# A four-layer hybrid denoising step on one core: 128-row contraction in every sample score matmul, and two layers' modulation vectors made in the retention layer

## The chip, the core and the metric

The kernel runs on one core of a Trainium2 chip. The metric is the device time of one execution in microseconds (us). The engines are TensorE (PE for matmuls, PEld for its weight loads), VectorE (DVE), ScalarE (ACT), GpSimd (POOL) and SyncE (SP, which here only issues DMAs).

## What is computed

Five token tiles of 128 rows (four of the sample, one of the prompt) go through four layers of width 1024: differential attention, retention, HGRN2, differential attention. Cut to what the change touches, the reference reads:

```python
def modulation(cvec, w, b):                       # once per layer and conditioning vector
    m = jax.nn.silu(cvec) @ w + b
    shift, scale, gate = jnp.split(m, 3, axis=-1)

def block(qblk):                                  # differential attention, 16 sub-heads of 64
    s = jnp.einsum('bqsd,bksd->bsqk', qblk, k)
    p = jax.nn.softmax(s, axis=-1).reshape(B, H, 2, Q_BLOCK, -1)
    a = p[:, :, 0] - lam * p[:, :, 1]
    return jnp.einsum('bhqk,bkhe->bqhe', a, v)

for l in range(DEPTH):
    h = rms_norm(x, g_pre[l]) * (1.0 + scale) + shift
    y = mixer[l % 3](h)
    x = x + gate * rms_norm(y, g_post[l])
```

Sample queries attend to 512 own keys and 128 cached keys (640 in all), after a rotary embedding; prompt queries attend to the 128 prompt keys.

## The kernel before

**Split products.** Matmul operands in the fp32r type carry only part of an fp32 number, so every operand is cut into a high and a low part (`whi`/`wlo`, `hh`/`hl`, `kh`/`kl`), and a product is three matmuls: high by high, high by low, low by high. `proj_b` (L248 to L250) makes 128 output columns for 320 tokens in 24 such matmuls, twice per column; `narrow` (L223 to L225) and `wide_unit` (L456 to L458) make 256 and 512 columns.

**Attention layers (0 and 3).** For each of 8 heads `diff_part` makes keys, then queries (`rope`, then `use` with L754 to L761: DVE, POOL, then an ACT copy of the high part at L760 and a DVE subtraction for the low part at L761). Each head has two sub-heads of 64 rows. Four SP DMAs (L732) copy `kh` into `kk`, which has a sub-head's 64 rows twice, one above the other; four more (L739) build `qq`, the sub-head's high part and low part stacked. So one 128-row matmul (L781) gives two of the three products. The third, high part of q by low part of k, is a 64-row matmul (L784). Per head and sample tile there are, for each sub-head, two of the one and two of the other (320 keys each), eight in all; 8 heads, 4 tiles and 2 layers make 64 such groups of eight. DVE takes the row maximum (L785), ACT the exponential (L787), and after `combine` PE turns the result (L811) and multiplies by v (L821). The prompt's scores (L793) have a form of their own.

`kh` and `q` are separate tiles with one buffer each; `kl`, `kk` and `qq` have two. The cached keys of all heads come by one 512 KB DMA per layer (`ck`, L665).

**Order.** PE's order is written by hand. `weave` runs a mixing generator (`diff_mix`, `ret_mix`, `hg_mix`) and a filling one (the next head's projections, then `tail`); each yields a number, and the filler is advanced until its numbers make up for the mixer's. A scheduler lays out the other engines, each of which then works in order. In `ret_mix` the yields between the stages are `RW` = 3.5, 9 and 11; in `hg_mix` they are 6, 1.5, 6, 1.5, 4 and 4.

**Modulation.** A layer's 3072 values for two conditioning vectors are 12 blocks of 256 columns (0 to 3 shift, 4 to 7 scale, 8 to 11 gate). A block is two DMAs of 512 KB (`mraw`, L312) and eight rows; a row is two operations, an ACT copy for the first row of the block (L357) and a DVE multiply-add for the others (L359, 14 per block), except that in attention layers every second row goes to ACT and POOL. `mod_turn` (L327 to L337) then turns the block on PE and finishes it with some small DVE operations into `modT`. Rows are called from `weave` at `mod_pace` rows per unit of filling: four times the loads queued for the layer, over `PACE[kind]`. In each layer the queue `modq` holds that layer's own gate blocks and the next layer's shift and scale blocks: 12 blocks in layers 0, 1 and 2, 4 in layer 3. `mod_finish` in `tail` does what is left. `modT` has two buffers.

Of the kernel before, what the change touches and what calls it, by code (L numbers as in the profile page):

```python
# [11 lines left out]
F32 = mybir.dt.float32  # L12
F32R = mybir.dt.float32r
# [8 lines left out]
P = 128  # L22
D = 1024
# [15 lines left out]
RW = (3.5, 9.0, 11.0, 0.5)  # L39
PACE = (155.0, 245.0, 195.0)  # L40
TOK = (0, 128, 384, 512, 256)

# [44 lines left out]
class Net:  # L87
# [227 lines left out]
    def mod_turn(self):  # L315

        nc = self.nc
        if self.modp is None:
            return
        l, b, acc = self.modp  # L320
        self.modp = None
        if b == 0:
            self.mods[l] = self.cp.tile([P, 24, 2], F32, tag="modT", bufs=2, name="modT")
        ps = self.one([P, 2, 2, P])
        for c in range(2):
            for j in range(2):
                nc.tensor.transpose(ps[:, c, j, :], acc[:, j, c * 128:c * 128 + 128], self.ident)  # L327
        r = slice(2 * b, 2 * b + 2)
        m = self.mods[l][:, r, :]
        wide = lambda a: a.unsqueeze(2).to_broadcast([P, 2, 2])  # L330
        nc.vector.tensor_reduce(out=m, in_=ps, axis=AX.X, op=ALU.add)
        nc.vector.tensor_tensor(out=m, in0=m, in1=wide(self.bmodT[:, l, r]), op=ALU.add)
        if 4 <= b < 8:
            nc.vector.tensor_scalar(out=m, in0=m, scalar1=1.0, scalar2=None, op0=ALU.add)
        if b >= 4:
            g = (self.gpre if b < 8 else self.gpost)[:, l, b % 4 * 2:b % 4 * 2 + 2]
            nc.vector.tensor_tensor(out=m, in0=m, in1=wide(g), op=ALU.mult)  # L337
# [305 lines left out]
    def diff(self, l, y):  # L643
# [3 lines left out]
        with tc.tile_pool(name=f"da{l}", bufs=2, reuse_waits="tile") as mp:  # L647
# [15 lines left out]
            nc.vector.tensor_scalar(out=nlam, in0=nlam, scalar1=-lam_init, scalar2=None, op0=ALU.add)  # L663
            ck = mp.tile([P, D], F32, bufs=1, name="ck")
            nc.sync.dma_start(ck, t["cache_k"][0, j].rearrange("s h d -> s (h d)"))  # L665
            st = types.SimpleNamespace(mp=mp, l=l, j=j, cc=cc, cs=cs, sub=sub, nlam=nlam, v={}, sg={}, ck=ck, q={}, k={})
            st.o, st.scored, st.done = {}, -1, -1
# [16 lines left out]
    def diff_part(self, st, kind, p):  # L684
# [27 lines left out]
        else:  # L712
            h = p
            kh = mp.tile([P, 640], F32R, tag="kh", bufs=1, name="kh")
            kl = mp.tile([P, 640], F32R, tag="kl", name="kl")
            kp = mp.tile([P, NP], F32, tag="kp", name="kp")

            def cached():
                pt = self.one([P, P])
                nc.tensor.transpose(pt, st.ck[:, h * 128:h * 128 + 128], self.ident)  # L720
                nc.scalar.activation(kh[:, 0:128], pt, AF.Copy)
                self.lo(kl[:, 0:128], pt, kh[:, 0:128], nc.vector)
# [4 lines left out]
            if h == 0:  # L727
                cached()
            kk = mp.tile([P, 2, 640], F32R, tag="kk", name="kk")
            for s in range(2):  # L730
                for r in range(2):
                    nc.sync.dma_start(kk[64 * r:64 * r + 64, s, :].bitcast(F32), kh[64 * s:64 * s + 64, :].bitcast(F32))  # L732
            q = mp.tile([P, 2, NS], F32R, tag="q", bufs=1, name="q")
            qp = mp.tile([P, NP], F32, tag="qp", name="qp")
# [9 lines left out]
            nc.sync.dma_start(t["new_k"][0, j].rearrange("s h d -> s (h d)")[:, h * 128:h * 128 + 128], ko)  # L744
            st.q[h], st.k[h] = (qq, qp), (kk, kl, kp)

# [19 lines left out]
    def diff_mix(self, st, y):  # L766
        nc, mp = self.nc, st.mp

        def scores(h, tt):
            (qq, qp), (kk, kl, kp) = st.q[h], st.k[h]  # L770
            nm = mp.tile([P, 2], F32, tag="nm", name="nm")
            sums = st.o[h][2][:, tt, :]
            pr = []
            if tt < 4:
                for s in range(2):
                    rows = slice(64 * s, 64 * s + 64)
                    sc = self.two()
                    qc = slice(tt * 128, tt * 128 + 128)
                    for c in range(2):
                        kc = slice(c * 320, c * 320 + 320)  # L780
                        nc.tensor.matmul(sc[:, c, :320], qq[:, s, qc], kk[:, s, kc], start=True, stop=False)  # L781
                    for c in range(2):
                        kc = slice(c * 320, c * 320 + 320)
                        nc.tensor.matmul(sc[:, c, :320], qq[rows, s, qc], kl[rows, kc], start=False, stop=True)  # L784
                    nc.vector.tensor_reduce(out=nm[:, s:s + 1], in_=sc[:, :, :320], axis=AX.XY, op=ALU.max, negate=True)  # L785
# [475 lines left out]
    def start(self, src):  # L1261
        nc, t = self.nc, self.t
        mm, tr = nc.tensor.matmul, nc.tensor.transpose
        mt = self.mods[0] = self.cp.tile([P, 24, 2], F32, tag="modT", bufs=2, name="modT")
        with self.tc.tile_pool(name="in0", bufs=1, reuse_waits="tile") as ip:
# [100 lines left out]
    def layers(self, depth):  # L1366
# [14 lines left out]
        for l in range(depth):  # L1381
# [3 lines left out]
            else:  # L1385
                self.x_out = [self.dp.tile([P, D], F32, tag=f"x{l}_{tt}", name=f"x{l}_{tt}") for tt in range(NT)]
            self.modq += [(l, b, i) for b in range(8, 12) for i in range(2)]
            if l + 1 < depth:
                self.modq += [(l + 1, b, i) for b in range(8) for i in range(2)]
            self.mod_pace, self.mod_pool = 4 * (len(self.modq) + len(self.modr)) / PACE[kind], None  # L1390
# [42 lines left out]
```

## Time and profile before

| what | value |
|---|---|
| median of 3 runs | 1962.97 us (1962.2 to 1963.04) |
| the profiled execution, its own time | 1961.53 us |
| its span, first to last instruction | 1959.7 us |
| PE busy | 1869.7 us, 95% |
| DVE busy | 1322.9 us, 68% |
| ACT busy, POOL busy | 982.8 us, 50%; 495.0 us, 25% |
| mean granted TensorE clock | 0.984 |

By their matmuls the layers lie at about 20 to 480 us (attention), 480 to 1060 (retention), 1060 to 1530 (HGRN2) and 1530 to 1960 (attention). A busy time is the time in which at least one instruction of the engine was under way; matmuls overlap, so the distance between two starts, not the duration, is what one matmul costs in a stream.

### The profile page before, as it was taken

The numbers are of one execution on the slowest core, as the hardware profiler recorded it, in microseconds if no ns is written. First come the engines' busy times: TensorE is split into PE (matmuls) and PEld (weight loads), VectorE is DVE, ScalarE is ACT, GpSimd is POOL, SyncE is SP. The second block draws the span as 40 slices with busy tenths as digits, with TensorE's granted clock in tenths as the row PEclk, the third lists the DMA queues.
The fourth block names the chain that finished last, engine by engine and source line by source line (L and its number), as shares of the span: only waits on it lengthen the run. The fifth ranks groups of instructions, "written<-read, shape, count | busy, mean of one in ns | idle before, by whom it ended". The sixth has DMA issues, their size and how long they took to land.

```text
span 1959.7 us, 31888 instructions
## 1 busy us (share of the span) xinstructions
PE 1869.7 (95%) x12060; PEld 1664.0 (85%) x12060; DVE 1322.9 (68%) x2553; ACT 982.8 (50%) x2271; POOL 495.0 (25%) x419
## 2 busy tenths in 40 slices
PE   6999999999899999999999999999889999999998
PEld 3789889977788888898787999999877889999976
DVE  4768788757766666544248788989765757666654
ACT  3556666555534434334334555555554545554552
POOL 0424343202222222222003232323221612211101
PEclk9999999999999999999999999999889999999999
DMA  9534444314343333223323333333214433323212
GB/s 301 163 109 116 115 124 130 91 56 151 124 131 110 120 120 115 83 65 124 119 77 120 102 91 103 103 103 103 83 43 158 136 100 94 87 80 84 81 52 101
DMA packets 224824, 214.08 MB, mean 109 GB/s; under 512 B 10416, under 2 KB 198688, under 8 KB 224672
## 3 DMA queue, kind: packets, MB, share of 16 engines
q1 hardware_dynamic: 224208, 211.67, 36.0%
q8 instruction: 95, 1.56, 0.3%
q14 instruction: 57, 0.47, 0.1%
q10 hardware_dynamic: 464, 0.39, 0.1%
HBM read 174.79 MB, written 18.35 MB: 99 GB/s over the span
## 4 chain that ended last, share of the span: by engine, by line
PE 71%; DVE 14%; ACT 4%; issue 4%; DMA 3%; POOL 2%; SPq 1%; DVEq 0%; POOLq 0%; ACTq 0%
PE one L456 8%; PE one L458 8%; PE one L457 8%; PE one L248 6%; PE one L249 6%; PE one L250 6%; DVE macc L359 3%; PE one L223 3%; PE one L821 3%; PE one L225 3%; PE two L784 3%; PE one L224 3%; PE two L781 2%; DVE wlo L114 2%; PE one L811 1%
## 5 line engine op out<-in xcount | busy, mean ns | idle before, releaser
L248 PE MATMUL one<-hh,whi 128*128 128x320 f32 x1152 | 372.2, 323 | 13.1 <-ACT qp L757 7.0
L249 PE MATMUL one<-hl,whi 128*128 128x320 f32 x1152 | 360.2, 313 | 0.0
L250 PE MATMUL one<-hh,wlo 128*128 128x320 f32 x1152 | 359.9, 312 | 0.0
L114 DVE TENSOR_TENSOR wlo<-raw,whi 128x1024 fp32r<-128x1024 f32 x192 | 245.2, 1282 | 135.3 <-ACT whi L176 133.8
L456 PE MATMUL one<-whi,hh 128*128 128x512 f32 x744 | 301.1, 405 | 3.4 <-ACT yo L552 2.4
L458 PE MATMUL one<-whi,hl 128*128 128x512 f32 x744 | 295.3, 397 | 0.5 <-DVE hl L114 0.5
L457 PE MATMUL one<-wlo,hh 128*128 128x512 f32 x744 | 295.7, 397 | 0.0
L176 ACT ACTIVATE whi<-raw 128x1024 fp32r<-128x1024 f32 x192 | 201.6, 1056 | 154.7 <-PE one L249 51.5
L359 DVE SCALAR_TENSOR_TENSOR macc<-mraw,smod,macc 128x256 f32<-128x256 f32 x432 | 233.2, 576 | 9.6 <-POOL macc L361 9.5
L248 PEld LDWEIGHTS one<-hh,whi 128*128 128x128 f32 x1152 | 220.9, 192 | 21.2 <-ACT qp L757 7.4
L249 PEld LDWEIGHTS one<-hl,whi 128*128 128x128 f32 x1152 | 220.8, 192 | 0.5
L250 PEld LDWEIGHTS one<-hh,wlo 128*128 128x128 f32 x1152 | 220.5, 191 | 0.3 <-DVE wlo L114 0.3
L223 PE MATMUL one<-whi,hh 128*128 128x256 f32 x720 | 212.4, 295 | 0.0
L225 PE MATMUL one<-whi,hl 128*128 128x256 f32 x720 | 203.1, 282 | 0.0
L224 PE MATMUL one<-wlo,hh 128*128 128x256 f32 x720 | 202.2, 281 | 0.0
L456 PEld LDWEIGHTS one<-whi,hh 128*128 128x128 f32 x744 | 140.8, 189 | 37.2 <-ACT yo L552 2.9
L458 PEld LDWEIGHTS one<-whi,hl 128*128 128x128 f32 x744 | 140.2, 188 | 35.3 <-DVE hl L114 2.1
L457 PEld LDWEIGHTS one<-wlo,hh 128*128 128x128 f32 x744 | 140.8, 189 | 29.8
L361 POOL TENSOR_TENSOR macc<-macc,mpart 128x512 f32<-128x512 f32 x64 | 93.7, 1466 | 191.8 <-ACT macc L357 75.8
L223 PEld LDWEIGHTS one<-whi,hh 128*128 128x128 f32 x720 | 135.8, 189 | 5.7 <-issue 4.2
L389 POOL TENSOR_TENSOR rs<-ms,mhalf 128x1 f32<-128x1 f32 (+1 forms) x72 | 65.9, 916 | 287.4 <-DVE ms L382 155.4
L224 PEld LDWEIGHTS one<-wlo,hh 128*128 128x128 f32 x720 | 136.5, 190 | 0.0
(344 smaller groups left out, 3709.9 us busy)
## 6 DMA issues: line engine op xcount, KB each, us to landing
mraw<-in_w_mod SPq DMA_DIRECT2D x96, 512.0 KB, 3.8
raw<-in_da_w_in SPq DMA_DIRECT2D x56, 512.0 KB, 4.2
raw<-in_hg_w_in SPq DMA_DIRECT2D x36, 512.0 KB, 4.0
raw<-in_ret_w_in SPq DMA_DIRECT2D x64, 256.0 KB, 3.1
kk<-kh SPq DMA_DIRECT2D x64, 160.0 KB, 3.6
qq<-q SPq DMA_DIRECT2D x64, 128.0 KB, 3.2
raw<-in_da_w_out SPq DMA_DIRECT2D x16, 512.0 KB, 4.0
raw<-in_ret_w_in SPq DMA_DIRECT2D x16, 512.0 KB, 3.9
```

The source lines that it names most:

```text
L114: return (eng or self.nc.gpsimd).tensor_tensor(out=out, in0=full, in1=hi.bitcast(F32), op=ALU.subtract)
L176: self.nc.scalar.activation(hi, raw, AF.Copy)
L223: mm(out, xh, wh[:, k % 4, :], start=(first and k == ks[0]), stop=False)
L224: mm(out, xh, wl[:, k % 4, :], start=False, stop=False)
L225: mm(out, xl, wh[:, k % 4, :], start=False, stop=(last and k == ks[-1]))
L248: nc.tensor.matmul(ps, wh[:, k, :], self.hh[:, k, c], start=(k == 0), stop=False)
L249: nc.tensor.matmul(ps, wh[:, k, :], self.hl[:, k, c], start=False, stop=False)
L250: nc.tensor.matmul(ps, wl[:, k, :], self.hh[:, k, c], start=False, stop=(k == KT - 1))
L359: nc.vector.scalar_tensor_tensor(out=m, in0=raw[:, k, :], scalar=c, in1=m, op0=ALU.mult, op1=ALU.add)
L456: mm(ps, xh, wh, start=(first and k == ks[0]), stop=False)
L457: mm(ps, xh, wl, start=False, stop=False)
L458: mm(ps, xl, wh, start=False, stop=(last and k == ks[-1]))
```

## The change

Five edits. The low part of k is stacked as the high part was: `kh` and `kl` become the halves of one tile `ks`, and four more DMAs per head make `kz`, the low part's 64 rows twice. The third product becomes a 128-row matmul of the whole `qq` by `kz` (it now also adds the low part of q by the low part of k), and the order within a sub-head is `kk`, `kz`, `kk`, `kz`. `ks` and `q` share one buffer (tag "split"). The cached keys come head by head (64 KB each, two buffers). The table `MOD_IN` puts 24 blocks into layer 1 (its own gate, all of layer 2, shift and scale of layer 3), none into layer 2 and layer 3's gate into layer 3; layer 0 is as before. `modT` gets a third buffer, and the space kept for DMA descriptors is set smaller.

```diff
+MOD_IN = (((0, range(8, 12)), (1, range(8))), ((1, range(8, 12)), (2, range(8)), (2, range(8, 12)), (3, range(8))), (),
+          ((3, range(8, 12)),))
...
-            self.mods[l] = self.cp.tile([P, 24, 2], F32, tag="modT", bufs=2, name="modT")
+            self.mods[l] = self.cp.tile([P, 24, 2], F32, tag="modT", bufs=3, name="modT")
...
-            kh = mp.tile([P, 640], F32R, tag="kh", bufs=1, name="kh")
-            kl = mp.tile([P, 640], F32R, tag="kl", name="kl")
+            ck = mp.tile([P, P], F32, tag="ck", name="ck")
+            nc.sync.dma_start(ck, t["cache_k"][0, j].rearrange("s h d -> s (h d)")[:, h * 128:h * 128 + 128])
+            ks = mp.tile([P, 2, 640], F32R, tag="split", bufs=1, name="ks")
+            kh, kl = ks[:, 0, :], ks[:, 1, :]
...
-            kk = mp.tile([P, 2, 640], F32R, tag="kk", name="kk")
-            for s in range(2):
-                for r in range(2):
-                    nc.sync.dma_start(kk[64 * r:64 * r + 64, s, :].bitcast(F32), kh[64 * s:64 * s + 64, :].bitcast(F32))
-            q = mp.tile([P, 2, NS], F32R, tag="q", bufs=1, name="q")
+            kk, kz = (mp.tile([P, 2, 640], F32R, tag=n, name=n) for n in ("kk", "kz"))
+            for both, src in ((kk, kh), (kz, kl)):
+                for s in range(2):
+                    for r in range(2):
+                        nc.sync.dma_start(both[64 * r:64 * r + 64, s, :].bitcast(F32), src[64 * s:64 * s + 64, :].bitcast(F32))
+            q = mp.tile([P, 2, NS], F32R, tag="split", bufs=1, name="q")
...
                     for c in range(2):
                         kc = slice(c * 320, c * 320 + 320)
                         nc.tensor.matmul(sc[:, c, :320], qq[:, s, qc], kk[:, s, kc], start=True, stop=False)
-                    for c in range(2):
-                        kc = slice(c * 320, c * 320 + 320)
-                        nc.tensor.matmul(sc[:, c, :320], qq[rows, s, qc], kl[rows, kc], start=False, stop=True)
+                        nc.tensor.matmul(sc[:, c, :320], qq[:, s, qc], kz[:, s, kc], start=False, stop=True)
...
-            self.modq += [(l, b, i) for b in range(8, 12) for i in range(2)]
-            if l + 1 < depth:
-                self.modq += [(l + 1, b, i) for b in range(8) for i in range(2)]
+            for m, bs in MOD_IN[l]:
+                if m < depth:
+                    self.modq += [(m, b, i) for b in bs for i in range(2)]
...
-    nc = _bacc.Bacc("TRN2", target_bir_lowering=False, num_devices=1)
+    nc = _bacc.Bacc("TRN2", target_bir_lowering=False, num_devices=1, dynamic_dma_scratch_size=1024)
```

PE, the first sample tile's scores of the first head in layer 0, between two projection matmuls. Before:

```order
L250 MATMUL one<-hh,wlo 128x320
L781 MATMUL two<-kk,qq 128x320 x2
L784 MATMUL two<-kl,qq 128x320 x2
L781 MATMUL two<-kk,qq 128x320 x2
L784 MATMUL two<-kl,qq 128x320 x2
L248 MATMUL one<-hh,whi 128x320
```

After:

```order
L252 MATMUL one<-hh,wlo 128x320
L783 MATMUL two<-kk,qq 128x320
L784 MATMUL two<-kz,qq 128x320
L783 MATMUL two<-kk,qq 128x320
L784 MATMUL two<-kz,qq 128x320
L783 MATMUL two<-kk,qq 128x320
L784 MATMUL two<-kz,qq 128x320
L783 MATMUL two<-kk,qq 128x320
L784 MATMUL two<-kz,qq 128x320
L250 MATMUL one<-hh,whi 128x320
```

The number of matmuls is the same; the two kinds now alternate, and all eight read 128 rows.

ACT, the start of layer 0, from head 0's queries on (`q` is the query's high part, `ko` the new key for the output, `kh<-one` or `ks<-one` head 1's cached keys, `kp` and `qp` the prompt's parts, `mpart` modulation). Before:

```order
L757 ACTIVATE qp<-one 128x64
L357 ACTIVATE mpart<-mraw,smod 128x256 x2
L760 ACTIVATE q<-t_745 128x256
L176 ACTIVATE whi<-raw 128x1024
L743 ACTIVATE ko<-one 128x128
L357 ACTIVATE mpart<-mraw,smod 128x256
L757 ACTIVATE qp<-one 128x64
L357 ACTIVATE mpart<-mraw,smod 128x256
L721 ACTIVATE kh<-one 128x128
L357 ACTIVATE mpart<-mraw,smod 128x256 x2
L760 ACTIVATE q<-t_785 128x256
L757 ACTIVATE kp<-one 128x64
```

After:

```order
L359 ACTIVATE mpart<-mraw,smod 128x256 x2
L178 ACTIVATE whi<-raw 128x1024
L746 ACTIVATE ko<-one 128x128
L359 ACTIVATE mpart<-mraw,smod 128x256
L760 ACTIVATE qp<-one 128x64
L359 ACTIVATE mpart<-mraw,smod 128x256 x3
L763 ACTIVATE q<-t_749 128x256
L763 ACTIVATE q<-t_789 128x256
L760 ACTIVATE kp<-one 128x64
L178 ACTIVATE whi<-raw 128x1024
L760 ACTIVATE kp<-one 128x64
L723 ACTIVATE ks<-one 128x128
```

Both writes of `q` have moved behind what stood after the first of them, and head 1's cached keys have moved behind both.

DVE, one head in the middle of the retention layer, from the last product of the scores to the state update (`s` from `cd` and `one`). Before:

```order
L359 SCALAR_TENSOR_TENSOR macc<-mraw,smod,macc 128x256 x2
L114 TENSOR_TENSOR vl<-one,vh 128x256
L359 SCALAR_TENSOR_TENSOR macc<-mraw,smod,macc 128x256
L619 SCALAR_TENSOR_TENSOR sg<-sg,one 128x256
L114 TENSOR_TENSOR vl<-one,vh 128x256
L619 SCALAR_TENSOR_TENSOR sg<-sg,one 128x256
L1021 SCALAR_TENSOR_TENSOR s_6574<-s_5831,cd,one 128x256 x2
```

After:

```order
L116 TENSOR_TENSOR vl<-one,vh 128x256
L361 SCALAR_TENSOR_TENSOR macc<-mraw,smod,macc 128x256 x3
L621 SCALAR_TENSOR_TENSOR sg<-sg,one 128x256
L361 SCALAR_TENSOR_TENSOR macc<-mraw,smod,macc 128x256 x4
L333 TENSOR_REDUCE modT<-one 128x4
L116 TENSOR_TENSOR vl<-one,vh 128x256
L361 SCALAR_TENSOR_TENSOR macc<-mraw,smod,macc 128x256
L334 TENSOR_TENSOR modT<-modT,par 128x4
L361 SCALAR_TENSOR_TENSOR macc<-mraw,smod,macc 128x256 x2
L621 SCALAR_TENSOR_TENSOR sg<-sg,one 128x256
L361 SCALAR_TENSOR_TENSOR macc<-mraw,smod,macc 128x256 x5
L1021 SCALAR_TENSOR_TENSOR s_6699<-s_5877,cd,one 128x256 x2
```

Where three multiply-adds of the modulation stood ahead of the state update, fifteen stand now. Counted over the five heads from the second to the sixth table of decays, DVE's order holds 140 such multiply-adds (30, 26, 28, 28, 28) and 28 small `modT` operations before, 271 (57, 55, 52, 57, 50) and 56 after, with some 43 other operations per head in both. In the HGRN2 layer none are left.

## Rows read from the trace of the kernel before

**Rows 1.** The page, section 1: busy us (share of the span) and instructions.

```profile
span 1959.7 us, 31888 instructions
PE 1869.7 (95%) x12060; PEld 1664.0 (85%) x12060; DVE 1322.9 (68%) x2553; ACT 982.8 (50%) x2271; POOL 495.0 (25%) x419
```

**Rows 2.** Stretches: length, busy PE, PEld, DVE, ACT, POOL; granted clock, DMA share, GB/s.

```profile
120.00:400.00 280.00, 275.83 (x1982) 252.58 (x1982) 222.57 (x467) 175.54 (x492) 99.89 (x79) 1.00 0.40 113
540.00:790.00 250.00, 249.17 (x1436) 221.31 (x1435) 169.20 (x355) 102.27 (x228) 62.83 (x49) 1.00 0.39 119
...
1175.00:1375.00 200.00, 184.26 (x1531) 179.98 (x1530) 177.56 (x313) 115.55 (x232) 59.60 (x43) 0.96 0.34 101
1600.00:1900.00 300.00, 298.82 (x2092) 270.25 (x2091) 193.84 (x423) 157.66 (x448) 53.49 (x48) 1.00 0.26 75
```

**Rows 3.** Timeline of PE in layer 0: start, length of the merged row, instruction.

```profile
209.93 0.46 PE L781 MATMUL two<-kk,qq 128*128 128x320 f32 x2
210.32 0.56 PE L784 MATMUL two<-kl,qq 64*128 64x320 f32 x2
210.81 0.56 PE L781 MATMUL two<-kk,qq 128*128 128x320 f32 x2
211.30 0.56 PE L784 MATMUL two<-kl,qq 64*128 64x320 f32 x2
211.78 0.39 PE L223 MATMUL one<-whi,hh 128*128 128x256 f32 x1
212.01 0.28 PE L224 MATMUL one<-wlo,hh 128*128 128x256 f32 x1
212.13 0.28 PE L225 MATMUL one<-whi,hl 128*128 128x256 f32 x1
```

**Rows 4.** Timeline of PE's weight loads in a projection stream of layer 0.

```profile
201.29 0.19 PEld L248 LDWEIGHTS one<-hh,whi 128*128 128x128 f32 x1
201.44 0.19 PEld L249 LDWEIGHTS one<-hl,whi 128*128 128x128 f32 x1
201.58 0.19 PEld L250 LDWEIGHTS one<-hh,wlo 128*128 128x128 f32 x1
```

**Rows 5.** PE's waits from 1120 to 1400 us: total, times, longest.

```profile
PE one L1213 <- ACT so L1226: 7.1, 2, 3.9
PE one L248 <- DVE sg L619: 6.0, 3, 2.3
PE one L327 <- ACT so L1226: 4.5, 2, 3.6
PE one L1219 <- ACT kt L1215: 2.5, 4, 1.4
```

**Rows 6.** Stretches of the HGRN2 layer at the lower clock, columns as in rows 2.

```profile
1176.80:1183.60 6.80, 4.41 (x18) 4.04 (x19) 6.80 (x17) 2.17 (x6) 0.73 (x1) 0.50 0.74 228
1275.80:1282.60 6.80, 4.84 (x20) 4.82 (x21) 4.78 (x12) 2.17 (x6) 0.73 (x1) 0.50 0.77 231
1371.40:1381.60 10.20, 7.04 (x29) 6.63 (x28) 6.98 (x13) 1.38 (x4) 1.72 (x2) 0.50 0.52 151
```

**Rows 7.** Instructions on macc alone by stretch, columns as in rows 2.

```profile
540.00:790.00 250.00, 5.39 (x36) 4.51 (x36) 71.26 (x138) 8.13 (x18) 0.00 (x0) 1.00 0.39 119
1175.00:1375.00 200.00, 5.87 (x32) 4.28 (x32) 66.93 (x115) 7.20 (x16) 0.00 (x0) 0.96 0.34 101
```

**Rows 8.** On modT alone: length, busy PE, PEld, DVE; granted clock, DMA share, GB/s.

```profile
540.00:790.00 250.00, 0.00 (x0) 0.00 (x0) 9.76 (x25) 1.00 0.39 119
```

**Rows 9.** Timeline of SP at two heads of layer 0: start, length of four issues.

```profile
89.23 2.61 SPq L732 DMA_DIRECT2D kk<-kh  x4
...
153.31 2.67 SPq L732 DMA_DIRECT2D kk<-kh  x4
```

**Rows 10.** Timeline of ACT at the same two heads: the first query copy.

```profile
91.37 0.42 ACT L760 ACTIVATE q<-t 128x256 fp32r<-128x256 f32 x1 [1.14 <-DVE t L759]
...
160.25 0.42 ACT L760 ACTIVATE q<-t 128x256 fp32r<-128x256 f32 x1 [0.87 <-DVE t L759]
```

**Rows 11.** The line of the kk copies: us from issue to landing.

```profile
DMA to landing us min/median/max: 2.4/3.6/5.4
```

More of the change, by code (lines that the diff above doesn't have):

```diff
@@ L663, in diff @@
             nc.vector.tensor_scalar(out=nlam, in0=nlam, scalar1=-lam_init, scalar2=None, op0=ALU.add)
-            ck = mp.tile([P, D], F32, bufs=1, name="ck")
-            nc.sync.dma_start(ck, t["cache_k"][0, j].rearrange("s h d -> s (h d)"))
-            st = types.SimpleNamespace(mp=mp, l=l, j=j, cc=cc, cs=cs, sub=sub, nlam=nlam, v={}, sg={}, ck=ck, q={}, k={})
+            st = types.SimpleNamespace(mp=mp, l=l, j=j, cc=cc, cs=cs, sub=sub, nlam=nlam, v={}, sg={}, q={}, k={})
             st.o, st.scored, st.done = {}, -1, -1
@@ L719, in cached @@
                 pt = self.one([P, P])
-                nc.tensor.transpose(pt, st.ck[:, h * 128:h * 128 + 128], self.ident)
+                nc.tensor.transpose(pt, ck, self.ident)
                 nc.scalar.activation(kh[:, 0:128], pt, AF.Copy)
@@ L744, in diff_part @@
             nc.sync.dma_start(t["new_k"][0, j].rearrange("s h d -> s (h d)")[:, h * 128:h * 128 + 128], ko)
-            st.q[h], st.k[h] = (qq, qp), (kk, kl, kp)
+            st.q[h], st.k[h] = (qq, qp), (kk, kz, kp)
     def rope(self, st, c0, hi, lo, pr, scale=1.0):
@@ L769, in scores @@
         def scores(h, tt):
-            (qq, qp), (kk, kl, kp) = st.q[h], st.k[h]
+            (qq, qp), (kk, kz, kp) = st.q[h], st.k[h]
             nm = mp.tile([P, 2], F32, tag="nm", name="nm")
@@ L775, in scores @@
                 for s in range(2):
-                    rows = slice(64 * s, 64 * s + 64)
                     sc = self.two()
@@ L1263, in start @@
         mm, tr = nc.tensor.matmul, nc.tensor.transpose
-        mt = self.mods[0] = self.cp.tile([P, 24, 2], F32, tag="modT", bufs=2, name="modT")
+        mt = self.mods[0] = self.cp.tile([P, 24, 2], F32, tag="modT", bufs=3, name="modT")
         with self.tc.tile_pool(name="in0", bufs=1, reuse_waits="tile") as ip:
```

## The prediction, made before the changed kernel ran

> **What bounds the kernel now.** I read the page's busy times first, then the stretches by layer, then PE's timeline where the change cuts, and last the waits. PE is busy 95% of the span, DVE 68% [rows 1], so PE is the first suspect everywhere; the stretches say where that is true [rows 2]. In the attention layers PE leaves 4.2 us of 280 idle in layer 0 (DVE 222.6 us, 79%) and 1.2 us of 300 in layer 3 (DVE 65%). In the retention layer it leaves 0.8 us of 250 idle (DVE 169.2 us, 68%). In the HGRN2 layer it is different: 15.7 us of 200 idle, at a granted clock of 0.96, while DVE is busy 177.6 us. So three layers are bound by PE, where only a cheaper stream of matmuls helps, and HGRN2 is bound by PE and DVE together: PE's own work there is about 200 - 15.7 - 6 (half of the busy time at the lower clock) = 178 us, and DVE needs as much.
>
> **Part 1, the score matmuls.** In a stream of 128-row matmuls of 320 columns the weight loads, and with them the matmuls, start 0.147 us apart [rows 4]. The eight score matmuls of one head and tile take from 209.93 to 211.78, 1.85 us or 0.23 each, and the matmul after them is followed at 0.23 us where the next of the same stream comes at 0.12 [rows 3]. Each change between a 128-row and a 64-row matmul delays itself and the matmul behind it. With all eight at 128 rows I expect eight stream steps, 1.18 us, and no delay behind: 0.67 + 0.11 = 0.78 us saved per group. There are 64 groups: -50 us of PE time. The work is PE's in two layers where PE is 98.5% and 99.6% busy, so it lies on the path. Bounds: -50, and +7 if nothing is gained (a pair of the 64-row kind costs 0.49 us, 0.245 each; eight at that price are 1.96 us).
>
> Giving back in layer 0: PE's 280 us shrink to about 255 while DVE's 222.6 stay, 87%. Between the two rows that I have (79% with 1.5% idle, and HGRN2's 100% with 22 us on 178, 12%) a straight line would give 5.5%, the flat part of a queue 2 to 3%. I take +6, bounds 0 to 14. Layer 3 comes to 194 of 275, 70%, as retention is now with 0.8 us idle: 0.
>
> **Part 2, kz and the shared buffer.** The four kk issues take SP 2.67 us and a copy lands 3.6 us after its issue, 5.4 at most [rows 9, 11]. Four kz issues follow, and `q` now lies in the buffer that all eight read, so ACT's first query copy waits for the last landing, with everything behind it on ACT: `ko`, the next `kp`, the exponentials and the copies of turned weights that PE waits for. In a head in the middle (kk from 153.31) the last kz issue would be near 158.0 and land at 161.6, at the latest 163.4; the copy ran at 160.25 [rows 9, 10]: 1.4 us late, at most 3.2. The new order has two or three instructions moved ahead of it, which hide most. For 14 such heads: +5, bounds 0 and 45. At the start of a layer there is no cover: kk from 89.23, so kz lands near 97.5, and the copy ran at 91.37, 6 us earlier; head 1's cached keys then wait for head 0's query copies in the same buffer, where before they waited only for kk. PE has a third of a head's projections queued there, and a wait of its own already. I take 4 per layer: +8, bounds 0 and 24 (twice 6, in two layers). The copies by head of the cached keys and the 64 kz issues cost SP some 0.65 us each (78 more issues, 51 us in two layers of some 450 each); the loads of weights behind them are two buffers ahead. If that cover were gone, a head's weights would come 2.7 us later, which is inside the bound of 45. The smaller space for descriptors and the third `modT` buffer cost nothing: no instruction of the two kernels differs by them.
>
> **Part 3, twelve blocks leave HGRN2.** They are 168 multiply-adds and their small `modT` operations; in 200 us of that layer macc takes DVE 66.9 of its 177.6 us [rows 2, 7]. Without it DVE needs about 105 us beside 178 of PE, 60%. The waits that end on DVE's queue, or on an ACT copy that waits for DVE's state updates, come to 20.1 us in the 280 us from 1120 [rows 5]. I let 18 of them go, what stays being the latency of the chain itself; and two more at the layer's end. The three stretches at the lower clock in the middle, each right after such a wait, hold 16.3 us of busy PE [rows 6], half of it lost: 8. Together -28, bounds -18 and -38.
>
> **Part 4, they arrive in retention.** DVE's order there holds, over five heads of some 50 us each, 271 multiply-adds for 140 and 56 small operations for 28. At 71.26 / 138 = 0.52 us each, and 9.76 / 25 = 0.39 for the small ones [rows 7, 8], that adds 131 x 0.52 + 28 x 0.39 = 79 us to 169.2: 248 us for a stretch in which PE works 249 [rows 2]. DVE is then asked for as much as in HGRN2 now. If retention pays as HGRN2 did, 12% of 250, it is +31, and with the sixth and seventh head +34; if it pays as layer 0 does at 79%, +4. The demand is nearest HGRN2's row, but its yields ahead of a reader are 9 and 11 where HGRN2 has some of 1.5, so a late DVE step finds more filling before PE needs it. I take +20, bounds +4 and +45. The ACT firsts (24) and the turning on PE move with it, at no net cost.
>
> **Sum**, against the profiled execution's 1961.5: -50 + 6 + 5 + 8 - 28 + 20 = -39, so 1922.5; the median of the runs shown lies 1.5 above that execution: **1924**.
>
> **Rivals.** *A, retention becomes a second HGRN2* (+34, and -24 there, since its tail keeps what it has): 18 us worse, about 1942. For it: DVE's demand of 99%, and fifteen multiply-adds ahead of a state update where three stood. Against: the longer yields. *B, DVE's added work is covered in retention as in layer 0, and the starts cost nothing*: +4 for +20 and 3 for 19 elsewhere, about 1892. For it: the multiply-adds wait for nobody and can slide. *C, slower: the shared buffer stops ACT for the whole landing in every head.* Each of the 14 heads pays 3.2 us and each layer's start 12: 45 + 24 in place of 13, which makes 1980. It decides from 52 us of such waits, some 3.2 us in each of 16 heads. For it: ACT works in order, and a copy of `at` for PE stands close behind. Against: the scheduler has put the query copy later already, and PE has other filling. *D, the change doesn't do what it says: the 128-row matmuls of one stationary tile come no closer than the 64-row pairs do now.* Then the scores give 0 to +7 and layer 0 gives nothing back: 1961.5 + 3 + 13 - 28 + 20 + 1.5, about 1971. A load would have to wait for the matmul before it in the same rows; in rows 4 loads of 0.19 us start every 0.147 us in the same 128 rows, so they overlap running matmuls. The Trainium skill, TensorE: Matmul & The Clock Gate, Part 3 (The mechanism), says that a weight load overlaps a running matmul only when their row groups differ; by that rule D holds, and the trace's rows 4 speak against it for a 128-row stream.
>
> **How the numbers follow.** The forecast, 1905 to 1935, has 0.50. A has 0.20 (1935 to 1957), B 0.13 (1885 to 1905), C 0.12 (from 1957 to 1985, by how many heads pay), D 0.05. This kernel's measurement tells about 0.2% from no change, 4 us. Below 1959: the forecast, A, B and a small part of C, 0.85; between 1959 and 1967 part of C, 0.05; above, the rest of C and D, 0.10. The range of 8 in 10 takes in A, most of B and the small end of C: 1892 to 1962.
>
> **What the profile after would show.** Right: the score group takes near 1.2 us and the matmul behind it steps at stream distance; HGRN2 has DVE near 60%, idle PE below 8 us in 400 and no lower clock in the middle; retention's DVE is above 90% with PE waits of 10 to 30 us that end on DVE (weights' low parts, state updates); ACT waits for kk or kz landings at two layer starts. Wrong: score matmuls still 0.23 us apart (D); ACT's waits on copies for several us in every head, with PE waiting for `at` (C); HGRN2's waits unchanged, which would make them latency and not DVE's queue; retention without PE waits (B).

## The result, and the profile after

The changed kernel takes **1913.05 us** (median of 4 runs, 1908.83 to 1915.52) against 1962.59 us for the kernel before in the same runs: ratio 0.9744, 95% interval 0.9729 to 0.9758. Run again unaltered, beside other kernels, it took 1910.48 us (0.9739, 0.9721 to 0.9757). The profiled execution, the lowest of the first four, took 1908.83 us at a mean granted clock of 0.989.

The page's first section answers to [rows 1], the stretches (layer 0, retention, HGRN2, layer 3) to [rows 2]; the columns are as there. Since the kernel is shorter, the last stretch ends at 1840.

```profile
span 1907.0 us, 32063 instructions
PE 1814.8 (95%) x12060; PEld 1651.2 (87%) x12060; DVE 1315.7 (69%) x2553; ACT 978.1 (51%) x2271; POOL 503.7 (26%) x419
```

```profile
120.00:400.00 280.00, 266.80 (x2003) 258.36 (x2002) 227.11 (x476) 175.01 (x498) 99.70 (x80) 0.99 0.46 130
...
540.00:790.00 250.00, 246.48 (x1437) 218.62 (x1437) 213.62 (x475) 108.08 (x243) 64.07 (x47) 1.00 0.49 152
1175.00:1375.00 200.00, 199.11 (x1736) 197.32 (x1735) 134.15 (x201) 127.78 (x254) 66.76 (x48) 1.00 0.23 67
1600.00:1840.00 240.00, 236.35 (x1798) 229.91 (x1797) 168.15 (x372) 132.77 (x380) 51.45 (x45) 1.00 0.38 104
```

PE's busy time fell by 55 us and its share stayed at 95%. In HGRN2 it is idle 0.9 us of 200 where it was 15.7, at full clock. In layer 0 it is idle 13.2 us of 280 where it was 4.2, and in retention 3.5 of 250 where it was 0.8. To see where the time went, the span is cut at events that both kernels have: first and last score of an attention layer, first and last turned key of retention, first and last turned decay of HGRN2. The columns are those of [rows 2]; first the kernel before, then after. The first two rows of each are layer 0 and layer 3, the last two retention and HGRN2.

```profile
104.30:424.90 320.60, 315.64 (x2208) 284.36 (x2206) 245.54 (x514) 193.93 (x544) 102.52 (x82) 1.00 0.38 106
1583.50:1898.20 314.70, 311.75 (x2175) 280.73 (x2174) 203.27 (x446) 164.40 (x465) 54.96 (x50) 1.00 0.28 79
...
535.90:911.00 375.10, 372.32 (x2168) 332.71 (x2167) 228.98 (x477) 153.56 (x345) 93.25 (x76) 1.00 0.35 109
1115.50:1457.20 341.70, 311.08 (x2540) 302.25 (x2539) 288.64 (x498) 203.26 (x409) 105.35 (x75) 0.95 0.30 89
```

```profile
98.00:412.50 314.50, 298.75 (x2207) 287.11 (x2208) 246.86 (x519) 191.92 (x547) 101.17 (x82) 0.98 0.44 124
1550.60:1846.40 295.80, 287.72 (x2176) 278.84 (x2175) 204.05 (x449) 162.47 (x468) 58.05 (x51) 1.00 0.37 101
...
524.40:911.70 387.30, 380.15 (x2216) 337.35 (x2215) 308.70 (x680) 163.72 (x369) 101.72 (x76) 1.00 0.44 138
1116.00:1424.90 308.90, 294.78 (x2493) 288.56 (x2491) 214.87 (x322) 195.73 (x391) 106.39 (x75) 0.97 0.22 65
```

| stage (us) | before | after | change | idle PE |
|---|---|---|---|---|
| up to layer 0's first score | 104.3 | 98.0 | -6.3 | |
| layer 0, its scores | 320.6 | 314.5 | -6.1 | 5.0 to 15.8 |
| retention | 375.1 | 387.3 | +12.2 | 2.8 to 7.2 |
| HGRN2 | 341.7 | 308.9 | -32.8 | 30.6 to 14.1 |
| layer 3, its scores | 314.7 | 295.8 | -18.9 | 3.0 to 8.1 |
| all else | 503.3 | 502.5 | -0.8 | |

PE's timeline at the group of scores that [rows 3] showed of before (layer 0, third head, last tile): start, length, instruction.

```profile
203.36 0.28 PE L227 MATMUL one<-whi,hl 128*128 128x256 f32 x1
203.48 0.31 PE L783 MATMUL two<-kk,qq 128*128 128x320 f32 x1
203.62 0.31 PE L784 MATMUL two<-kz,qq 128*128 128x320 f32 x1
...
204.35 0.31 PE L783 MATMUL two<-kk,qq 128*128 128x320 f32 x1
204.50 0.31 PE L784 MATMUL two<-kz,qq 128*128 128x320 f32 x1
204.65 0.28 PE L225 MATMUL one<-whi,hh 128*128 128x256 f32 x1
204.77 0.28 PE L226 MATMUL one<-wlo,hh 128*128 128x256 f32 x1
```

Eight score matmuls now take 203.48 to 204.65, 1.17 us, each 0.147 us behind the one before, and the projection behind them goes on at its own 0.12. Over all 64 groups the median from first start to the start behind the last fell from 1.89 to 1.25 us, the sum from 120.9 to 81.3 us, and the step behind the group from 0.25 to 0.145 us: 39.6 + 6.8, some 46 us of PE's time. (The medians are above the 1.17 shown because 31 groups stand behind matmuls of another kind, turned modulation or v by turned weights; their first step is 0.23 us, before as after.)

In layer 0 the waits look like this: who waited, for whom, us in total, times, longest. First PE, then ACT.

```profile
PE one L821 <- ACT at L814: 9.8, 13, 2.4
PE one L811 <- DVE pe L863: 2.7, 2, 2.4
PE two L783 <- DMA qq<-q: 2.6, 1, 2.6
```

```profile
ACT mpart L359 <- POOL macc L363: 15.6, 17, 2.8
ACT at L813 <- PE one L811: 11.2, 12, 2.2
ACT q L763 <- DMA kz<-ks: 7.5, 7, 1.5
```

Most of PE's new waiting is for `at`, ACT's copy of the turned weights (9.8 us where before had 2.7). ACT is hardly idle during these waits: `at` stands in its queue behind exponentials, weight copies and modulation copies. Earlier in the queue ACT itself stood still, for POOL to free an `mpart` buffer (15.6 us in the layer) and for `kz` to land before a query copy (7.5 us). The longest wait for `at` (what ACT did, then PE's wait and the clock after it):

```profile
186.62 0.91 ACT L359 ACTIVATE mpart<-mraw,smod 128x256 f32<-128x256 f32 x2 [0.39 <-POOL macc L363]
187.44 0.78 ACT L787 ACTIVATE pe<-two,nm 128x640 f32<-128x640 f32 x1
188.21 1.04 ACT L178 ACTIVATE whi<-raw 128x1024 fp32r<-128x1024 f32 x1
189.15 0.78 ACT L787 ACTIVATE pe<-two,nm 128x640 f32<-128x640 f32 x1
190.40 0.28 ACT L814 ACTIVATE at<-one 128x128 f32<-128x128 f32 x1
```

```profile
190.73 0.58 PE L821 MATMUL one<-v,at 128*128 128x128 f32 x1 [2.42 <-ACT at L814]
```

```profile
190.20:193.80 3.60, 3.07 (x13) 3.07 (x14) 3.46 (x8) 1.73 (x8) 0.00 (x0) 0.53 0.32 57
```

After this wait of 2.4 us PE runs at the lower of its two levels for 3.4 us (granted clock 0.53 over the 3.6 us shown). The stage of layer 0 has three such stretches now (from 98, 190 and 279 us), and before it had none; they hold 10.3 us of busy PE, about half of it lost. The other two follow waits of 2.6 us, for `qq` at the first score, and of 2.4 us, for DVE at a turning. The first has a counterpart before: there a stretch of 6.8 us (from 88 us) lies just ahead of the first score, where after has none, so a part of what the stage loses the start gains.

### The profile page after: what moved, and what is told of

The parts are those of the page before. It is cut to its first block, busy times and chain, and to the rows that moved or that the text cites. A ratio compares the mean times of both kernels' runs of the same rounds, so it can differ in the third digit from the quotient of the medians.

```text
span 1907.0 us, 32063 instructions
## 1 busy us (share of the span) xinstructions
PE 1814.8 (95%) x12060; PEld 1651.2 (87%) x12060; DVE 1315.7 (69%) x2553; ACT 978.1 (51%) x2271; POOL 503.7 (26%) x419
## 4 chain that ended last, share of the span: by engine, by line
PE 57%; DVE 20%; ACT 8%; DMA 5%; issue 4%; POOL 3%; SPq 2%; DVEq 0%; ACTq 0%; POOLq 0%
PE one L458 7%; PE one L460 7%; PE one L459 7%; PE one L250 4%; PE one L251 4%; PE one L252 4%; DVE macc L361 4%; DVE wlo L116 3%; PE one L821 3%; PE one L225 3%; PE one L226 2%; PE one L227 2%; ACT whi L178 2%; DMA kz<-ks 1%; DVE nm L785 1%
## 5 line engine op out<-in xcount | busy, mean ns | idle before, releaser
L250 PE MATMUL one<-hh,whi 128*128 128x320 f32 x1152 | 365.4, 317 | 9.3 <-ACT qp L760 6.4
L361 DVE SCALAR_TENSOR_TENSOR macc<-mraw,smod,macc 128x256 f32<-128x256 f32 x432 | 216.3, 544 | 10.2 <-POOL macc L363 9.6
L225 PE MATMUL one<-whi,hh 128*128 128x256 f32 x720 | 207.8, 289 | 0.0
```

The costliest lines, as they stand in the source:

```text
L225: mm(out, xh, wh[:, k % 4, :], start=(first and k == ks[0]), stop=False)
L250: nc.tensor.matmul(ps, wh[:, k, :], self.hh[:, k, c], start=(k == 0), stop=False)
L361: nc.vector.scalar_tensor_tensor(out=m, in0=raw[:, k, :], scalar=c, in1=m, op0=ALU.mult, op1=ALU.add)
```

## The experiments

**The two parts apart.** `score_only` is the changed kernel with the old place of the modulation blocks; `mod_only` is the kernel before with the new place, the third `modT` buffer and the smaller descriptor space.

```diff
# score_only, against after
-MOD_IN = (((0, range(8, 12)), (1, range(8))), ((1, range(8, 12)), (2, range(8)), (2, range(8, 12)), (3, range(8))), (),
+MOD_IN = (((0, range(8, 12)), (1, range(8))), ((1, range(8, 12)), (2, range(8))), ((2, range(8, 12)), (3, range(8))),
```

> The changed kernel with the table of blocks as before the change (12 blocks in each of layers 0, 1, 2): only the scores' part of the change is in. Theory (two separate gains: 64 groups of score matmuls at 1.25 us for 1.89 and one faster matmul behind each, some 47 us of TensorE time, of which layer 0 gives back most of its half because ACT and DVE come late there): 1932 us, 25 to 35 below the kernel before, retention and HGRN2 as before (375 and 342 us between their first and last head). Rival (the two parts help each other, the lighter HGRN2 layer is what lets the scores' gain through): under 20 below.

> The kernel before with the new table of blocks and the third modT buffer alone; its scores have 64-row matmuls and kl. Theory: 1942 us, 17 to 25 below the kernel before: HGRN2 about 33 shorter, retention about 12 longer. Rival (retention loses as much as HGRN2 gains once DVE is asked for all of its time there): within 5 of the kernel before.

`score_only` took 1933.1 us (ratio 0.9837, 0.982 to 0.9854), 31 us less than before, as expected: its layers 0 and 3 take 315.8 and 296.7 us, and HGRN2 stays at 342.3. `mod_only` took 1930.83 (0.9834, 0.9818 to 0.985), 33.5 us less and better than the theory's 1942: retention 386.6 us, 11.5 more, as that theory had it, HGRN2 305.4, 36.3 less where it had 33. The rest of the miss are an earlier start and a shorter layer 3, which the theory had at nothing. Added up the two would be 65 us, and the change is 50. Five of the difference are an earlier start of layer 0 that both show (97.9 and 99.7 us where before had 104.3), which is taken up below; HGRN2 (305.4 alone, 308.9 together) and layer 3, where `mod_only` gained 2.9 us of its own, make some 5 more, and the last 5, unexplained, are of the size by which the medians of such runs differ.

**The row form alone.** `rows64` is the changed kernel with the third product back on 64 rows of `kz`, in the old order.

```diff
+                    rows = slice(64 * s, 64 * s + 64)
...
-                        nc.tensor.matmul(sc[:, c, :320], qq[:, s, qc], kz[:, s, kc], start=False, stop=True)
+                    for c in range(2):
+                        kc = slice(c * 320, c * 320 + 320)
+                        nc.tensor.matmul(sc[:, c, :320], qq[rows, s, qc], kz[rows, s, kc], start=False, stop=True)
```

> The changed kernel with the third product on 64 rows again, in the old order kk kk, kz kz; kz, its four DMAs, the shared buffer and the block table stay. Theory (the row form is the gain): a score group takes 1.85 to 1.89 us again and layers 0 and 3 lose what they gained, 1940 to 1948 us. Rival (the order of the other engines or the freed kl made the gain): 1910 to 1918.

`rows64` took 1941.9 us (0.9887, 0.9872 to 0.9902); its groups take 1.92 us again, its attention layers 322.9 and 315.4. So the row form is worth some 30 us of time, 8 in layer 0 and 20 in layer 3. And all the rest of part 2 (`kz`, the shared buffer, the cached keys by head) costs 11 us beside the old row form: `rows64` against `mod_only`.

**What the 128 rows do that an order can't.** `grouped64` keeps `kz` and makes all four 128-row products of a group first and then the four 64-row ones. `grouped_kl` does the same to the kernel before (with the new place of the blocks): no `kz`, no stacked low part, no shared buffer.

```diff
# grouped_kl, against before (the same lines in grouped64, with kz[rows, s, kc] for kl[rows, kc])
+                scs = [self.two() for _ in range(2)]
                 for s in range(2):
...
+                        nc.tensor.matmul(scs[s][:, c, :320], qq[:, s, qc], kk[:, s, kc], start=True, stop=False)
+                for s in range(2):
...
+                        nc.tensor.matmul(scs[s][:, c, :320], qq[rows, s, qc], kl[rows, kc], start=False, stop=True)
```

> The changed kernel with the third product on 64 rows, and with both sub-heads' four 128-row matmuls first and the four 64-row ones after them: one change of row form inside a group instead of three. Theory (a change of form delays two matmuls, the one that changes and the next; a run of one form goes at 0.147 us): a group takes 1.45 to 1.60 us, the time lies 1922 to 1932 us. Rival (a 64-row matmul costs 0.25 us whatever stands beside it): 1.65 us or more, 1932 to 1942 us.

> The kernel before with the new block table, and with a tile's four 128-row score matmuls first and then the four 64-row ones on kl, which needs no kz, no shared buffer and no DMA more. Theory (in that order two 64-row matmuls of different halves run side by side, so a group takes 1.25 us as with 128 rows, but both maxima come late): a group 1.25 us, the time between the changed kernel with this order (1921) and the changed kernel (1911), some 1914 us. Rival (the late maxima cost what the form gains): 1925 to 1931, as with the block table alone.

`grouped64` took 1921.51 us (0.9798, 0.9784 to 0.9811), half a us below the theory's bounds, and its group takes 1.25 us, under the 1.45 of the theory and the 1.65 of the rival and no more than with eight at 128 rows. PE's timeline of `grouped_kl` shows why:

```profile
203.40 0.74 PE L782 MATMUL two<-kk,qq 128*128 128x320 f32 x4
204.07 0.56 PE L787 MATMUL two<-kl,qq 64*128 64x320 f32 x4
204.56 0.38 PE L225 MATMUL one<-whi,hh 128*128 128x256 f32 x1
204.79 0.28 PE L226 MATMUL one<-wlo,hh 128*128 128x256 f32 x1
```

Four 64-row matmuls take 204.07 to 204.56, 0.49 us, what two took in [rows 3]. By the median starts over 64 groups they start in pairs, 5 to 7 ns apart, and the next pair 0.25 us later. The rows shown don't name the half that a matmul reads, but the trace's semaphore records settle it: in the program the second matmul of each half carries the signal that releases that half's row maximum, and in all 64 groups of both kernels the two signals are on the second pair. So a pair is one matmul of each half, running side by side, and the third in the program starts before the second. What is left against 128 rows is the step behind the group, 0.25 us in place of 0.145, and that both row maxima of DVE come at the end of the group; in the two attention layers PE is idle 7 us more than in the change in `grouped64`, and no more in `grouped_kl`. `grouped_kl` took 1915.05 (0.9758, 0.9741 to 0.9776), 2 to 5 us from the change: it has the change's times in the two attention layers (315.4 and 296.3 us) without the 64 `kz` copies. So most of what the scores' part of the change brought can be had without stacking the low part, by leaving the alternation: 15.8 us beside `mod_only`, where the change has 18 to 20. The stacked form can bring more than the order does once its buffer is not shared, as the next run shows.

**The shared buffer.** `unshared` gives `ks` and `q` buffers of their own.

```diff
-            ks = mp.tile([P, 2, 640], F32R, tag="split", bufs=1, name="ks")
+            ks = mp.tile([P, 2, 640], F32R, tag="ks", bufs=1, name="ks")
...
-            q = mp.tile([P, 2, NS], F32R, tag="split", bufs=1, name="q")
+            q = mp.tile([P, 2, NS], F32R, tag="q", bufs=1, name="q")
```

> The changed kernel with ks and q in buffers of their own, so that the query copy doesn't wait for the kz landings and the next head's key copy not for qq. Theory (layer 0's waits for at end on ACT because modulation work, not the query copy, stands before it): 1909 to 1915 us, layer 0's idle TensorE time stays above 8 us. Rival (the shared buffer stops ACT and so TensorE in every head): 1895 to 1904, idle time in layer 0 back to some 5 us.

> The changed kernel unaltered, so that the next variants stand beside it on the same chip. Both theories: 1909 to 1916 us.

The change run again took 1910.48 us, as expected. `unshared` took 1903.93 us (0.9689, 0.9671 to 0.9707): 6.6 to 9.1 below the two medians of the change, and 27 below `mod_only`. The time is the rival's, the idle time the theory's. Gone are ACT's waits for `kz`, PE's 2.6 us for `qq` at the first score, and this wait of the change, for head 1's cached keys:

```profile
99.05 0.28 ACT L723 ACTIVATE ks<-one 128x128 fp32r<-128x128 f32 x1 [5.18 <-DMA qq<-q]
```

But most of layer 0's idle time stays:

```profile
96.70:407.00 310.30, 297.02 (x2206) 285.57 (x2207) 245.31 (x516) 191.17 (x544) 103.16 (x82) 0.99 0.45 126
```

```profile
PE one L821 <- ACT at L814: 8.6, 12, 2.4
```

PE is idle 13.3 us of the stage where the change had 15.8. So the buffer is a part of the loss, and `at` is late mostly for another reason.

**What makes `at` late.** First a guess at one wait: ACT stands 15.6 us behind POOL for an `mpart` buffer. `unsh_mpart4` gives four of them to `unshared`.

```diff
-                part = pool.tile([P, 2, 256], F32, tag="mpart", bufs=2, name="mpart")
+                part = pool.tile([P, 2, 256], F32, tag="mpart", bufs=4, name="mpart")
```

> The variant with ks and q in buffers of their own, and four buffers instead of two for mpart, the half of the modulation that ACT makes and POOL adds. Theory (what is left of layer 0's TensorE waits ends on ACT copies that stand behind an mpart copy, which waits for POOL to free a buffer): ACT's waits for POOL there fall from 14 us to under 5, TensorE's waits for at from 8.6 to under 5, and the time lies 3 to 6 us below the variant with two buffers. Rival (the copies wait for the row maximum and for the turned weights, DVE's and TensorE's own chain): within 2 us.

Theory and rival fell: 1913.93 us (0.9755, 0.9737 to 0.9772), 10 us slower than `unshared`. The wait on POOL is gone from ACT's list, and another stands in its place:

```profile
ACT mpart L359 <- DMA mraw<-in_w_mod: 26.9, 14, 3.0
```

I read it so: the copies ahead go sooner, and then ACT stands at the next one until its weights land, with `at` behind it; PE's wait for `at` is 11.1 us in 12. A wait taken away at one buffer came back, longer, at the next.

Then the whole work: `nomod0` leaves layer 0's twelve modulation blocks out (constants stand for their values), and only layer 0 is read from it.

```diff
-        if b == 0:
+        if b == 0 and l > 1:
...
-            for m, bs in MOD_IN[l]:
+            if l == 0:
+                self.mods[1] = self.cp.tile([P, 24, 2], F32, tag="modT", bufs=3, name="modT")
+                nc.vector.memset(self.mods[1], 0.5)
+                nc.vector.memset(self.mods[0][:, 16:24, :], 0.5)
+            for m, bs in MOD_IN[l] if l > 0 else ():
```

> The changed kernel with the modulation work of layer 0 left out (its 12 blocks: layer 0's gate and layer 1's shift and scale are constants, so what is computed is not the reference's and the outputs are others); it is read for layer 0 alone, from its first to its last score matmul. Theory (layer 0's remaining idle TensorE time, some 16 of 314 us, is ACT, DVE and POOL being held up by modulation): idle falls under 8 us and the stage to 296 us or less (layer 3 with 4 blocks has 8 of 296). Rival (the chain from scores through maximum, exponential and turning limits it by itself): idle stays above 11 us and the stage above 301.

```profile
93.20:383.60 290.40, 286.07 (x2160) 278.65 (x2159) 190.34 (x424) 156.16 (x452) 45.65 (x42) 0.99 0.37 99
```

```profile
PE one L821 <- ACT at L814: 1.0, 2, 0.7
```

The stage takes 290.4 us, PE is idle 4.3 of them, and the waits for `at` are 1.0 us where the change had 9.8, though ACT still waits 6.0 us for `kz`. So the modulation is what PE waits for in layer 0 once its matmuls are shorter. The run takes out its work on DVE, ACT and POOL, its loads and its 7.2 us of turning on PE all at once (the turning shortens the stage, not the idle time); that the engines' work and not the loads makes `at` late is argued from ACT's queue, not shown.

**Where the blocks should lie.** `unsh_bal20` and `unsh_bal16` are `unshared` with 20 or 16 of the 24 blocks in retention and 4 or 8 in HGRN2.

```diff
# unsh_bal20
-MOD_IN = (((0, range(8, 12)), (1, range(8))), ((1, range(8, 12)), (2, range(8)), (2, range(8, 12)), (3, range(8))), (),
-          ((3, range(8, 12)),))
+MOD_IN = (((0, range(8, 12)), (1, range(8))), ((1, range(8, 12)), (2, range(8)), (2, range(8, 12)), (3, range(4))),
+          ((3, range(4, 8)),), ((3, range(8, 12)),))
```

> The same variant with 20 blocks in the retention layer and 4 (layer 3's scale) in the HGRN2 layer. Theory (retention loses about 5 us to DVE's load beside 6 for the turning itself): retention's first to last head 3 to 5 us shorter, HGRN2's 2 to 4 us longer, the time within 3 us of the variant with 24. Rival (retention's 12 us are DVE's load, growing steeply at its end): retention 8 us shorter or more, the time 4 to 8 us lower.

> The variant with ks and q in buffers of their own, with 16 blocks in retention and 8 (layer 3's shift and scale) in HGRN2. Theory (retention's DVE queue is empty enough with 20 already; the turning moves one for one): retention 3 to 5 us shorter than with 20, HGRN2 4 to 7 us longer, the time 1898 to 1902 us. Rival (retention still pays for load): 1890 to 1896.

`unsh_bal20` took **1898.59 us** (0.968, 0.9666 to 0.9693), the lowest of all that do the whole work, though its interval overlaps that of `unshared`: retention 381.9 us where `unshared` has 389.2, HGRN2 312.5 where it has 307.5. Retention's 7.3 us lie between theory and rival, HGRN2's 5.0 above the theory's bounds. `unsh_bal16` took 1906.59 (0.971, 0.969 to 0.973), above theory and rival: against `unsh_bal20` retention is only 2.0 us shorter and HGRN2 6.1 longer; the other 4 us between the two medians lie outside these stages. The same 200 us of HGRN2 in the two, `unsh_bal20` first:

```profile
1175.00:1375.00 200.00, 198.20 (x1686) 196.53 (x1685) 144.57 (x224) 130.98 (x259) 67.86 (x48) 1.00 0.24 70
```

```profile
1175.00:1375.00 200.00, 193.93 (x1641) 191.57 (x1640) 159.19 (x263) 127.32 (x257) 66.83 (x48) 0.99 0.29 85
```

With the rows of after and before, DVE's share in this layer is 67, 72, 80 and 89%, and PE's idle time 0.9, 1.8, 6.1 and 15.7 us: in these four rows flat up to some 70% and steep behind it.

**The earlier start.** In all profiles of changed kernels layer 0's first score comes at 93 to 100 us, in that of before at 104.3. `before_scratch` is the kernel before with the smaller descriptor space alone.

```diff
-    nc = _bacc.Bacc("TRN2", target_bir_lowering=False, num_devices=1)
+    nc = _bacc.Bacc("TRN2", target_bir_lowering=False, num_devices=1, dynamic_dma_scratch_size=1024)
```

> The kernel before with the smaller space for DMA descriptors (1024) alone; nothing else is changed. The question is the first score of layer 0, which comes at 104.3 us in the profiled execution of before and at 96.6 to 99.7 us in every profile of a changed kernel, all of which have the smaller space and some of which change nothing else ahead of it but the order of a few instructions. Theory, an accident of the one profiled execution: the time is that of before, 1960 to 1966, and the first score may come anywhere from 97 to 104. Rival, the space itself: the loads of the first 40 us move faster (314 and 356 GB/s in the first two stretches of 20 us where before had 295 and 308), the first score comes at 97 to 100 and the time is 4 to 7 us below before, 1956 to 1959.

1963.47 us (0.9997, 0.9989 to 1.0006): no gain, and the first score at 103.1 us. So the space doesn't move the start; and two late starts in two profiles without the other changes, against none in twelve with them, speak against an accident. What differs is how fast the first loads go. From the DMA view of the first 45 us (all packets; then KB each and median us from issue to landing), `before_scratch` and `mod_only`:

```profile
DMA packets 19613, 13.64 MB, mean 303 GB/s; under 512 B 559, under 2 KB 18972, under 8 KB 19612
...
mraw<-in_w_mod SPq DMA_DIRECT2D x18, 512.0 KB, 7.6
```

```profile
DMA packets 22094, 14.90 MB, mean 331 GB/s; under 512 B 604, under 2 KB 21452, under 8 KB 22092
...
mraw<-in_w_mod SPq DMA_DIRECT2D x18, 512.0 KB, 6.4
```

The same loads in the same order on SP land 1.2 us sooner in the median. In both kernels every engine works through the same instructions in the same order up to 541 us, so until there they differ in the layout alone. What the faster kernels share beyond the space is the third `modT` buffer of 192 bytes, which moves every buffer allocated behind it: by the built programs the first `mraw` buffer lies at byte 121,088 in them (a multiple of 256), at 120,896 in `before_scratch` and 136,256 in before (both 64 bytes past one). Other buffers moved by the same 192 bytes; which of them matters, and why, no run shows.

## Why the prediction was right, and where its terms were off

The time, 1913, lies in the range, 11 us below the forecast of 1924: faster, by the mechanism named, cheaper scores and an HGRN2 freed of DVE's load. Its terms didn't all hold, and that the sum is so near is partly luck: misses of 14 us on one side and 28 on the other.

- **Part 1, -50 us of PE: held**, 46 by the groups' own times. Rival D fell: matmuls of one stationary tile come 0.147 us apart, as the stream in [rows 4] does. So the rule of the Trainium skill, TensorE: Matmul & The Clock Gate, Part 3 (The mechanism), that a weight load overlaps a running matmul only when their row groups differ, doesn't hold for this stream; the same section also allows it for loads into a background weight buffer, which D left out.
- **Layer 0's give-back, +6, and 0 in layer 3: the worst term.** Of 46 us of PE the two layers kept 25 (6.1 and 18.9). Idle PE rose by 10.8 and 5.1 us, and lower-clock stretches took about 5 more. The step that failed is the choice of the flat part: I took 2 to 3% for layer 0 with DVE at 87% of PE's own work, where the straight line gave 5.5%. The load came as forecast, 86% in the 280 us, but PE lost 6.3% of its work there, 13.2 us idle and some 3 to the clock. Layer 0's stage gave back 17 of its 23 us, beyond the bound of 14; `unshared` gives back 13, so some 4 are the buffer's. `nomod0` names what lies behind the rest: the modulation. Layer 3, which I had at nothing, has 5.1 us more of idle time.
- **The shared buffer, +5 in the middle and +8 at the starts: the sum was near, the split was not.** `rows64` against `mod_only` gives 11 for all of part 2, `unshared` 6.6 to 9.1 for the buffer. ACT's waits for `kz` are 13.5 us in 12 in both layers, none over 2.8, where rival C wanted 52: that refutes C. At layer 0's start head 1's cached keys wait 5.2 us and PE 2.6 us for `qq`; that doesn't show in the start itself, which came 6.3 us sooner for another reason, mostly the layout.
- **"The third `modT` buffer cost nothing": wrong in sign.** Some 5 us of earlier start came with the new layout (4.6 in `mod_only`). That no instruction differs didn't mean that no time does.
- **HGRN2, -28: held**, -32.8. What was late, DVE's queue, went; some 7.3 us of the gain (by retention's rows below) are the turning of twelve blocks on PE, which I had called no net cost: over the two layers it is none, but it belongs to both terms. Without it this one is 25.5. Of the signs named for it, the full clock in the layer's middle came, and idle PE under 8 us did not: it is 14.1 us in the stage, 8 of them in the last 25 us, where a lower-clock stretch stays, too.
- **Retention, +20: too high**, +12.2. These rows are of instructions on `macc` alone, before and after, in the whole stage:

```profile
535.90:911.00 375.10, 6.59 (x44) 5.51 (x44) 72.27 (x140) 9.02 (x20) 0.00 (x0) 1.00 0.35 109
```

```profile
524.40:911.70 387.30, 13.86 (x92) 11.23 (x92) 150.99 (x308) 20.04 (x44) 0.00 (x0) 1.00 0.44 138
```

PE's own turning is 7.3 of the 12.2 us; the waits that I priced at 20 came to 4.4 us of idle PE. DVE was asked for less than I had worked out: 168 multiply-adds and 36 small operations raised its busy time by 79.7 us, 0.39 each, where I took 0.50 each; by themselves they account for 78.7 and 15.3 us, so the durations of back-to-back operations overlap and don't add. And I put the count of five heads into a row of 250 us, while five heads last 267 us before and 281 after: the 250 us from 540 hold 100 multiply-adds more, not 131. DVE is busy 85% of them and not 99%. So rival A fell with its premise, and B, which priced retention at +4, had the waits right. The signs named for this layer, DVE above 90% and 10 to 30 us of PE's waits ending on DVE, didn't come: 6.6 us of such waits.

In the profiled executions the sum came to -52.7 where -39 was forecast. The attention layers' scores kept 14 less (-25 where -50 + 6 + 5 stood), and the starts, retention and HGRN2 gave 15, 8 and 5 more. What remains open: which buffer's address makes the first loads faster, and why HGRN2 takes some 3 us more with both parts than with the second alone; its stage then has 17.1 us at the lower clock where `mod_only` has 10.2, and 1.2 us more of idle PE. The best version seen is `unsh_bal20`; joining it to `grouped_kl`'s order was not tried.

## What to carry to other kernels

When a bound engine's work shrinks, look first at who feeds it: here a layer with 1.5% of idle PE had a second engine at 79%, and there most of the saving of matmul time was given back, as waits and as stretches at the lower clock. Work moved to another layer takes all its engines along: count its share on the bound engine at full price, and the rest by the distance of starts in a busy queue, not by durations. And before stacking data to make all matmuls one shape, try the order that groups the shapes: it gave 15.8 us for no data at all, where the stacked form gave 18 to 20, and 27 only with buffers of its own.

## What the runs showed of the hardware

Of four 64-row matmuls behind one another, two on each half of the rows, those on different halves ran side by side, even past one of the same half that stands between them in the program: pairs of 320 columns start 5 to 7 ns apart, one pair every 0.25 us. Two of the same half start 0.25 us apart. A change between 128 and 64 rows costs about 0.09 us at the matmul that changes (0.235 for 0.147), and behind a change back to 128 rows the next matmul costs 0.10 us more (0.25 for 0.147). And the loads of the first 45 us moved 331 GB/s or 303 GB/s by a change of layout alone, with the same DMAs in the same order; which property of the layout does it stays open.
